# A two-block transformer kernel: a later silu on another load queue, a pace of the modulation steps by stage, and six smaller reorderings

## The chip, the core and the metric

The kernel runs on one core of a Trainium2 chip. A core has TensorE (PE: matmuls; PEld is its weight load), VectorE (DVE), ScalarE (ACT), GpSimd (POOL) and SyncE (SP), each with an instruction stream of its own, run in order; they meet through semaphores. Transfers between HBM and the core's memory are issued by SP or ACT here, each on a queue of its own, and are carried by 16 DMA engines. The metric is the device time of one execution in microseconds (us). In the trace every row has its engine, the line of the kernel it stems from, and the idle time ahead of it with what ended that.

## What is computed

Two blocks of two layers, float32 in and out, 256 tokens of width 1024. The parts that the change touches, cut:

```python
def mixer_block(h, ...):                       # block 1, both layers
    proj = (h @ w_in)                          # conv, retention, GLA and gate columns
    y_a = short_conv(cu, cb, cc, conv_w)
    y_b = head_norm(retention(rq, rk, rv), ret_gn_w, center=True) * silu(rg)
    gate_logits = ga_down @ gla_w_a2 + gla_b_a
    log_a = log_sigmoid(gate_logits) / 16
    y_c = head_norm(gated_linear_attention(gq, gk, gv, log_a), gla_gn_w) * silu(gr)
    merged = (sigmoid(gate_a) * (y_a @ w_branch_a) + sigmoid(gate_b) * (y_b @ w_branch_b)
              + sigmoid(gate_c) * (y_c @ w_branch_c))
    return merged @ w_out
# block 1, per layer: x += norm(mixer(norm(x)));  x += norm(swiglu(norm(x)))

# block 2, per layer, for a latent x and a context xc of 256 tokens each:
    mod_x = silu(c) @ ada_w[l] + ada_b[l]      # 6 x 1024 values; the same of c_ctx for the context
    hx = rmsnorm(x) * (1 + sc1) + sh1
    mix = conv branch, mLSTM, attention (8 query heads, 2 key heads of 64), gated, @ w_out
    x = x + g1 * mix
    x = x + g2 * conv_ffn(rmsnorm(x) * (1 + sc2) + sh2)
```

## The kernel before

Activations stay in on-chip memory, transposed: 1024 features as 8 tiles of 128, 256 tokens along the free axis, two tiles to a buffer (128x512). Only weights stream. A chunk of 128x1024 float32 (512 KB) is fetched on SP by `load` (L188; five buffers, `raw`); `halve` splits it into two float32r halves, `whi` on ACT (L197) and `wlo` on DVE (L199), and `mmT` runs 24 matmuls on it: high weight by high activation (L214), low by high (L218), high by low (L220). `mmK` (L228, L230, L232) is the same with the roles of the operands exchanged. So one chunk asks PE for 24 passes, ACT for one split, DVE for one.

Work is written down as a sequence of chunks; the scheduler of the framework orders each engine's instructions from it, with priorities (`high_priority`; `soon` is one of them) and explicit after-relations (`issue_after`). Side work (GLA decay and levels, retention, normalisations) runs in generators in lanes: `later` puts one in a lane, every chunk's `tick` moves each lane one step, `drain` runs a lane to its end.

Block 1, each layer: `b1_norm` splits the scaled input into `xh` and `xl` and forms the squares for the norm in `b1_norm_rest`; the mixer (L700 to 830) multiplies chunk after chunk of `w_in`, starts the lanes, then runs the branch stage (`gates`, `branch`: three branches of four column pairs, from L803 on), then `w_out`. `gla_decay` (L853) forms the decay from `ga` by the matmul `gl` (L866). `gla_scores` (L884) has eight levels; each makes E = exp(-|cum - ref| / 16) on DVE (L902, L903) and ACT (L904), the products `ql` (DVE, L906) and `kl` (POOL, L907), the matmuls `gs` (L922) and masked copies of them on DVE (L930). `gn_finish` (L935) normalises the heads: mean, square, variance, then `rsqrt` (L239 to L244), eleven DVE instructions on 128x4 values. The swiglu FFN follows, 22 column tiles and then `down`.

The modulation of block 2's layers is computed meanwhile, beside block 1: its input `silu` (128 x 2 x 1024, the vector repeated over partitions) is loaded on ACT's queue and made by tanh in `ada_prep` (L353). Each `ada_step` (L366) loads one 512 KB chunk of `ada_w` on SP, through the same five buffers, and runs two multiply-and-reduce instructions on DVE (L376), behind the latest `wlo`. `ada_beat` makes a step at every `ada_every`-th weight chunk; `ada_pace(n)` sets that number, up to a goal of 48 steps before block 2's first layer. Before: every second chunk in layer 0's FFN, every eighth in layer 1's mixer, every second in layer 1's FFN.

In block 2, an attention block of two heads (`r` = 0, 1) multiplies scores by values into one PSUM tile `po` (L1455), head r into partitions 64r to 64r+63, `nk` = 4 key tiles for the latent and 2 for the context; each matmul is two passes. The last FFN ends with four pairs of `down` (22 row tiles in three chunks by two column tiles), each followed by the residual (`b2_residual`, L1814) and a store.

## Time and profile before

| | us |
|---|---|
| median of 3 runs | 2595.44 |
| lowest, highest | 2587.75, 2596.06 |
| the profiled execution's own time | 2584.17 |
| its span in the profile | 2581.5 |
| PE busy | 2524.3 (98%) |
| DVE busy | 1949.0 (75%) |
| ACT busy | 1282.6 (50%) |
| POOL busy | 144.4 (6%) |

The span runs from the first to the last instruction of the trace; 2.7 us lie around it. Busy times are sums over the instructions of an engine. A row of the timeline gives the start, the length and, in brackets, the idle time of that engine just ahead of it. The windows give the same sums for a stretch, and the TensorE clock that was granted there (1.00 is 2.4 GHz, 0.50 is 1.2 GHz).

### The profile page before, as it was taken

To read this page: it belongs to the slowest core of one execution; us is meant where nothing else is said; L and a number is where in the kernel's file an instruction comes from. 1 tells how busy PE (TensorE), PEld (TensorE's weight loads), DVE (VectorE), ACT (ScalarE), POOL (GpSimd) and SP (SyncE) were. 2 spreads that over 40 slices of the span, in tenths; PEclk is the share of its full clock that TensorE was granted. 3 is DMA by queue.
4 is the path that set the end of the run, shared out by engine and by line. 5 is a ranking of instruction groups with operands and counts; after the bars stand their busy time and mean duration, and the time that the engine had idled before them with its cause. 6 is when DMAs were issued, how large, how long until landed. Compare 5 with 4: busy or idle time off the path is not lost. (4 is left out here: it accounts for less than half of the span.)

```text
span 2581.5 us, 44809 instructions
## 1 busy us (share of the span) xinstructions
PE 2524.3 (98%) x18010; PEld 2319.6 (90%) x18010; DVE 1949.0 (75%) x3254; ACT 1282.6 (50%) x2003; POOL 144.4 (6%) x151
## 2 busy tenths in 40 slices
PE   7999999999999999999999999999999999999999
PEld 7999999999999999888977679988889899999999
DVE  6987799699869958876884456975677674966994
ACT  5545544553454546343444534642345644665763
POOL 0100000010100001000010110000000000000000
PEclk9999999999999999999999999999999999999999
DMA  6545488554656754322333224434336333444554
GB/s 232 172 165 180 146 266 258 188 196 149 206 177 212 263 182 168 114 90 90 107 102 111 74 107 148 167 124 141 115 127 203 136 106 121 141 131 155 178 190 148
DMA packets 116209, 405.62 MB, mean 157 GB/s; under 512 B 12817, under 2 KB 16529, under 8 KB 116001
## 3 DMA queue, kind: packets, MB, share of 16 engines
q1 hardware_dynamic: 112880, 397.96, 46.0%
q10 hardware_dynamic: 3120, 4.80, 0.5%
q8 instruction: 141, 2.31, 0.4%
q14 instruction: 68, 0.55, 0.1%
HBM read 401.66 MB, written 1.05 MB: 156 GB/s over the span
## 5 line engine op out<-in xcount | busy, mean ns | idle before, releaser
L199 DVE TENSOR_TENSOR wlo<-raw,whi 128x1024 fp32r<-128x1024 f32 (+3 forms) x674 | 816.0, 1215 | 353.9 <-ACT whi L197 352.2
L197 ACT ACTIVATE whi<-raw 128x1024 fp32r<-128x1024 f32 (+3 forms) x674 | 697.7, 1040 | 591.8 <-PE pj L220 222.3
L214 PE MATMUL pj<-hh,whi 128*128 128x256 f32 (+1 forms) x3120 | 528.8, 311 | 5.5 <-ACT whi L197 4.0
L218 PE MATMUL pj<-hh,wlo 128*128 128x256 f32 (+1 forms) x3120 | 523.5, 309 | 4.3 <-DVE wlo L199 3.7
L214 PEld LDWEIGHTS pj<-hh,whi 128*128 128x128 f32 x3120 | 437.3, 188 | 46.2 <-ACT whi L197 5.2
L218 PEld LDWEIGHTS pj<-hh,wlo 128*128 128x128 f32 x3120 | 435.6, 189 | 43.4 <-DVE wlo L199 8.1
L220 PE MATMUL pj<-hl,whi 128*128 128x256 f32 (+1 forms) x2440 | 389.0, 296 | 0.0
L220 PEld LDWEIGHTS pj<-hl,whi 128*128 128x128 f32 x2440 | 329.6, 188 | 17.5 <-issue 0.3
L376 DVE CUSTOM_DVE_ANT_0 adr<-raw,silu 128x1024 bf16<-128x1024 f32 x192 | 238.1, 1245 | 0.5
L220 PE MATMUL pj<-kc,whi 128*128 128x512 f32 (+1 forms) x680 | 151.8, 344 | 0.0
L1263 DVE SCALAR_TENSOR_TENSOR dw<-z,hw,dw 128x512 f32<-128x512 f32 (+1 forms) x240 | 135.9, 609 | 0.2
L220 PEld LDWEIGHTS pj<-kc,whi 128*128 128x128 f32 x680 | 112.2, 188 | 16.7
L1821 ACT ACTIVATE fc<-pj,vecs 128x256 f32<-128x256 f32 (+1 forms) x78 | 52.0, 667 | 113.9 <-PE pj L220 111.3
L228 PE MATMUL pk<-whi,hh 128*128 128x256 f32 (+1 forms) x512 | 88.0, 291 | 0.0
L1822 DVE SCALAR_TENSOR_TENSOR fc<-pj,vecs,fc 128x255 f32<-128x255 f32 (+1 forms) x78 | 47.4, 609 | 48.7 <-ACT fc L1821 47.9
L230 PE MATMUL pk<-wlo,hh 128*128 128x256 f32 (+1 forms) x512 | 83.7, 283 | 0.0
L218 PE MATMUL dn<-fah,wlo 128*128 128x256 f32 (+1 forms) x440 | 76.5, 301 | 0.9 <-DVE wlo L199 0.9
L214 PE MATMUL dn<-fah,whi 128*128 128x256 f32 (+1 forms) x440 | 76.7, 301 | 0.0
L220 PE MATMUL dn<-fal,whi 128*128 128x256 f32 (+1 forms) x440 | 76.5, 300 | 0.1
L228 PEld LDWEIGHTS pk<-whi,hh 128*128 128x128 f32 x512 | 72.5, 190 | 3.0 <-issue 0.7
L255 POOL TENSOR_TENSOR sq<-sq,sq 128x512 f32<-128x512 f32 x15 | 25.2, 1681 | 855.5 <-ACT sq L252 642.8
L214 PE MATMUL pj<-yh,whi 128*128 128x256 f32 (+1 forms) x384 | 71.5, 313 | 0.0
(432 smaller groups left out, 3686.2 us busy)
## 6 DMA issues: line engine op xcount, KB each, us to landing
raw<-stream SPq DMA_DIRECT2D x620, 512.0 KB, 3.6
raw<-ada_stream SPq DMA_DIRECT2D x96, 512.0 KB, 3.9
raw<-stream SPq DMA_DIRECT2D x36, 384.0 KB, 3.5
raw<-stream SPq DMA_DIRECT2D x11, 408.0 KB, 3.2
raw<-stream SPq DMA_DIRECT2D x6, 272.0 KB, 2.7
xc<-xT SPq DMA_DIRECT2D x2, 512.0 KB, 5.6
xc<-cT ACTq DMA_DIRECT2D x1, 1024.0 KB, 10.9
silu<-c ACTq DMA_DIRECT2D x2, 512.0 KB, 12.6
```

The lines of the kernel that those rows point to most:

```text
L197: nc.scalar.activation(hi, raw, AF.Copy)
L199: self.mark = nc.vector.tensor_tensor(out=lo, in0=raw, in1=hi.bitcast(F32), op=ALU.subtract)
L214: mm(out, wh[:, k, cs], xh[k], start=first and k == 0, stop=False)
L218: mm(out, wl[:, k, cs], xh[k], start=False, stop=False)
L220: mm(out, wh[:, k, cs], xl[k], start=False, stop=last and k == kt - 1)
L228: mm(out, xh[k], wh[:, k, :], start=first and k == 0, stop=False)
L230: mm(out, xh[k], wl[:, k, :], start=False, stop=False)
L255: nc.gpsimd.tensor_tensor(out=sqs[0], in0=sqs[0], in1=sq, op=ALU.add)
L376: nc.vector.tensor_tensor_reduce(junk, raw, self.silu[:, s], 0.5, 0.0, ALU.mult, ALU.add, self.mods[:, l, n, s : s + 1])
L1263: V.scalar_tensor_tensor(d, src, w, d, ALU.mult, ALU.add)
L1821: A.activation(v(t), v(ps), AF.Identity, scale=w(1), bias=self.col(f"ffn_conv_b{l}", f + i))
L1822: V.scalar_tensor_tensor(v(t)[..., 1:256], v(ps)[..., 0:255], w(0), v(t)[..., 1:256], ALU.mult, ALU.add)
```

## The change

1. Six matmuls on constants are put at the head of PE's stream.
2. `ada_prep` is parted: the two `silu` loads (`ada_load`) stay where they were in the program but go to SP's queue; the tanh and the multiply move to the start of layer 0's branch stage.
3. The pace: every fourth chunk in the branch stages of both layers, every third in the FFNs, none in the rest of the mixers.
4. `b1_norm`: the `xl` instructions lose their priority, and the squares are put behind the last weight split on ACT (`self.high`).
5. GLA level: min(-e, e) on DVE becomes an Abs on ACT, with the sign in the scale of the Exp.
6. `gn_finish`: `rsqrt` on DVE becomes one power on POOL.
7. The value products of two heads alternate.
8. The last pair of `down` runs one column tile after the other; each is added and stored when it is done, the last in two halves on two queues.

```diff
@@ halve
-            nc.scalar.activation(hi, raw, AF.Copy)
+            self.high = nc.scalar.activation(hi, raw, AF.Copy)
@@ ada_prep
+    def ada_load(self):
+        for s in range(2):
+            self.nc.sync.dma_start(self.silu[:, s], self.d["c2"][s : s + 1].to_broadcast([128, 1024]))
...
-            v = self.silu[:, s]
-            nc.scalar.dma_start(v, self.d["c2"][s : s + 1].to_broadcast([128, 1024]))
...
@@ b1_norm, b1_norm_rest
-        with self.soon():
-            for j, (hi, lo) in enumerate(hl):
+        for j, (hi, lo) in enumerate(hl):
...
-        with self.soon():
+        with self.soon(), self.tc.issue_after(self.high.ins):
             parts = self.squares([self.x_pair(j) for j in range(4)])
@@ down
-    def down(self, l, j, H, L, name):
+    def down(self, l, j, H, L, name, done=None):
         ps = self.mm("dn")
+        if done:
+            for a in range(2):
+                p = ps[:, a * 256 : a * 256 + 256]
+                for r, kt in ((0, 8), (8, 8), (16, 6)):
+                    w = self.chunk(name, l, r * 128, kt, (2 * j + a) * 128, 128)
+                    self.mmT(p, w, H[r : r + kt], L[r : r + kt], first=r == 0, last=r == 16)
+                    self.tick()
+                done(a, p)
+            return
@@ mixer of block 1, start
-            self.ada_prep()
+            self.ada_load()
...
-        else:
-            self.ada_pace(8)
@@ mixer of block 1, ahead of the branch stage
+        if l == 0:
+            self.ada_prep()
+        self.ada_pace(4, 1)
@@ FFN of block 1
-        self.ada_pace(2, 1)
+        self.ada_pace(3, 1)
@@ gla_scores
-                V.scalar_tensor_tensor(e, e, -1.0, e, ALU.mult, ALU.min)
-                A.activation(e, e, AF.Exp, scale=1.0 / 16)
+                A.activation(e, e, AF.Abs)
+                A.activation(e, e, AF.Exp, scale=-1.0 / 16)
@@ gn_finish
-            self.rsqrt(y, v, 4)
+            nc.gpsimd.tensor_tensor(out=y, in0=v, in1=self.mhalf[:, 0:4], op=ALU.pow)
@@ attention
-            for r in range(2):
-                for k in range(nk):
+            for k in range(nk):
+                for r in range(2):
@@ last FFN of block 2
-        for j in range(4):
+        for j in range(3):
             ps = self.down(l, j, H, L, "ffn_w_down_2")
...
+        def done(a, ps):
+            k = 6 + a
+            for i in range(1 + a):
+                c = slice(256 * i // (1 + a), 256 * (i + 1) // (1 + a))
+                x = self.xc[:, k, c]
+                V.scalar_tensor_tensor(x, ps[:, c], self.mods[:, l, 40 + k, 0:1], x, ALU.mult, ALU.add)
+                (self.nc.scalar if i else self.nc.sync).dma_start(self.d["outT"][128 * k : 128 * k + 128, c], x)
+        self.down(l, 3, H, L, "ffn_w_down_2", done)
@@ start of the program
+            ps = self.aux("warm")
+            for _ in range(6):
+                nc.tensor.matmul(ps[:, 0:256], self.ones, self.one256, start=True, stop=True)
```

How the scheduler places this is seen at three places. First ACT in layer 0's mixer, some 25 to 50 us into the program: `whi` are splits, `gm`, `rmask` and `cT` loads of masks and of the context on ACT's queue, `ga` feeds the matmul `gl`. Before:

```order
L416 DMA xc<-cT 128x8x256 [waits DMAHW6_49]
L197 ACTIVATE whi_443<-raw_441 128x1024 [waits DMAHW4_49,PE_49]
L197 ACTIVATE whi_488<-raw_486 128x1024 [waits PE_49]
L709 ACTIVATE gv_416<-pk_152,rs_234 128x256 [waits Pool_49]
L709 ACTIVATE gv_416<-pk_153,rs_234 128x256 [waits DVE_49]
L357 DMA silu<-c 128x1024 [waits DMAHW0_49]
L357 DMA silu<-c 128x1024 [waits DMAHW2_49]
L197 ACTIVATE whi_525<-raw_523 128x1024 [waits PE_49]
L361 ACTIVATE adr_422<-silu 128x512 [waits DMAHW0_49]
L361 ACTIVATE adr_425<-silu 128x512 [waits DVE_49]
L361 ACTIVATE adr_429<-silu 128x512 [waits DMAHW2_49,DVE_49]
L361 ACTIVATE adr_432<-silu 128x512 [waits DVE_49]
L860 ACTIVATE ga_471<-ga_472 16x256 [waits DVE_49,PE_49]
```

After (the two loads of `silu` now stand in SP's stream, each between two weight loads):

```order
L415 DMA gm_350<-gmask 128x512 [waits DMAHW5_49]
L418 DMA kc_130<-rmask 128x512 [waits DMAHW6_49]
L418 DMA kc_131<-rmask 128x512 [waits DMAHW7_49]
L419 DMA xc<-cT 128x8x256 [waits DMAHW0_49]
L197 ACTIVATE whi_438<-raw_436 128x1024 [waits DMAHW3_49,PE_49]
L197 ACTIVATE whi_483<-raw_481 128x1024 [waits PE_49]
L721 ACTIVATE gv_423<-pk_159,rs_241 128x256 [waits Pool_49]
L721 ACTIVATE gv_423<-pk_160,rs_241 128x256
L197 ACTIVATE whi_520<-raw_518 128x1024 [waits PE_49]
L873 ACTIVATE ga_466<-ga_467 16x256 [waits PE_49]
```

The two loads and the four tanh no longer stand ahead of `ga`; the waits of the mask and context loads on DMA semaphores are on other semaphores than before, since the count of loads on each has shifted.

Second, DVE in the mixers, where `gn_finish` of a retention half (`var`, `rsh`, `on`) meets the masked copies `S` of a GLA level. Before:

```order
L199 TENSOR_TENSOR wlo_1744<-raw_1741,whi_1743 128x1024
L242 TENSOR_TENSOR rst_1570<-rsh_1569 128x4
L579 TENSOR_TENSOR yal_1585<-cy_1477,yah_1584 128x512
L243 SCALAR_TENSOR_TENSOR rst_1570<-rst_1570,var_1566 128x4
L947 TENSOR_TENSOR on_1619<-ro_1516,mu_1620 128x512
L244 SCALAR_TENSOR_TENSOR rsh_1569<-rst_1570,rsh_1569 128x4
L930 COPY_PREDICATED S_602<-Am_125,gs_1643 128x2x128
L242 TENSOR_TENSOR rst_1570<-rsh_1569 128x4
L930 COPY_PREDICATED S_603<-Am_125,gs_1643 128x2x128
L243 SCALAR_TENSOR_TENSOR rst_1570<-rst_1570,var_1566 128x4
L953 TENSOR_REDUCE var_1626<-sq_1624 128x4
L244 SCALAR_TENSOR_TENSOR rsh_1569<-rst_1570,rsh_1569 128x4
```

After:

```order
L199 TENSOR_TENSOR wlo_1717<-raw_1714,whi_1716 128x1024
L581 TENSOR_TENSOR yal_1569<-cy_1472,yah_1568 128x512
L960 TENSOR_TENSOR on_1603<-ro_1511,mu_1604 128x512
L943 COPY_PREDICATED S_597<-Am_132,gs_1616 128x2x128
L943 COPY_PREDICATED S_598<-Am_132,gs_1616 128x2x128
L966 TENSOR_REDUCE var_1610<-sq_1608 128x4
L943 COPY_PREDICATED S_597<-Am_132,gs_1617 128x2x128
L967 TENSOR_SCALAR var_1610<-var_1610 128x4
L943 COPY_PREDICATED S_598<-Am_132,gs_1617 128x2x128
L970 TENSOR_TENSOR on_1603<-on_1603,rsh_1613 128x512
```

The multiply chains of `rsqrt` between splits and copies are gone; `on` reads the `rsh` that POOL has written.

Third, PE at the first value products of the latent in block 2, with the scores of the next heads behind them. Before (x2 is two passes with the same head):

```order
L1455 MATMUL po_15752<-pT_15532,vt_13152 64x256 x2
L1455 MATMUL po_15752<-pT_15533,vt_13120 64x256 x2
L1455 MATMUL po_15752<-pT_15534,vt_13152 64x256 x2
L1455 MATMUL po_15752<-pT_15535,vt_13120 64x256 x2
L1435 MATMUL sc_15769<-kT_13153,qT_14324 128x256
```

After:

```order
L1468 MATMUL po_15671<-pT_15451,vt_13071 64x256
L1468 MATMUL po_15671<-pT_15453,vt_13071 64x256
L1468 MATMUL po_15671<-pT_15451,vt_13071 64x256
L1468 MATMUL po_15671<-pT_15453,vt_13071 64x256
L1468 MATMUL po_15671<-pT_15452,vt_13039 64x256
L1468 MATMUL po_15671<-pT_15454,vt_13039 64x256
L1468 MATMUL po_15671<-pT_15452,vt_13039 64x256
L1468 MATMUL po_15671<-pT_15454,vt_13039 64x256
L1448 MATMUL sc_15688<-kT_13072,qT_14243 128x256
```

The four key tiles are the same; `pT` of the two heads (`15451`, `15452` of the one, `15453`, `15454` of the other) now alternate from matmul to matmul.

## Rows read from the trace of the kernel before

**Rows 1.** Section 1 of the page: each engine's busy time, its share of the span, instructions.
```profile
PE 2524.3 (98%) x18010; PEld 2319.6 (90%) x18010; DVE 1949.0 (75%) x3254; ACT 1282.6 (50%) x2003; POOL 144.4 (6%) x151
```

**Rows 2.** Waits of TensorE over the span: total us, times, longest us.
```profile
PE pk L655 <- ACT xh L497: 8.8, 3, 7.5
...
PE gl L866 <- ACT ga L860: 3.7, 1, 3.7
...
PE gs L922 <- DVE rsh L244: 2.5, 1, 2.5
...
PE rsb L296 <- DVE dg L289: 2.4, 5, 0.5
...
PE st L273 <- DVE sq L259: 1.0, 3, 0.5
```

**Rows 3.** Timeline of ScalarE near the start: start, length, instruction, [idle before <- releaser].
```profile
42.54 1.15 ACT L361 ACTIVATE adr<-silu 128x512 f32<-128x512 f32 x2 [9.26 <-DMA silu<-c]
...
45.62 0.36 ACT L860 ACTIVATE ga<-ga 16x256 f32<-16x256 f32 x1
```

**Rows 4.** Timeline of TensorE over the same place.
```profile
46.02 2.07 PE L866 MATMUL gl<-ga,kc 16*128 16x256 f32 x4 [3.69 <-ACT ga L860]
...
48.02 1.22 PE L228 MATMUL pk<-whi,hh 128*128 128x256 f32 x4
```

**Rows 5.** Two stretches: length, busy time of each engine, granted clock, DMA share, GB/s.
```profile
45.50:52.34 6.84, 6.32 (x24) 5.48 (x25) 6.36 (x12) 5.09 (x8) 0.00 (x0) 0.50 0.36 118
...
612.10:618.96 6.86, 5.59 (x25) 5.39 (x26) 6.17 (x20) 0.74 (x2) 0.00 (x0) 0.50 0.23 76
```

**Rows 6.** DMA issues between 29 and 46 us: KB each, median us from issue to landing.
```profile
raw<-stream SPq DMA_DIRECT2D x4, 512.0 KB, 8.4
...
silu<-c ACTq DMA_DIRECT2D x2, 512.0 KB, 12.6
```

**Rows 7.** Timeline of TensorE at three waits in the two mixers of block 1.
```profile
113.00 0.70 PE L986 MATMUL rs<-r,r 128*128 128x256 f32 x2 [1.03 <-DVE r L746]
...
149.68 0.88 PE L965 MATMUL ot<-mats,on 128*128 128x128 f32 x6 [0.61 <-DVE on L957]
...
613.37 2.04 PE L922 MATMUL gs<-ql,kl 64*128 64x128 f32 x8 [2.47 <-DVE rsh L244]
```

**Rows 8.** Five stretches of block 1, columns as in group 5.
```profile
580.00:632.00 52.00, 48.27 (x386) 46.44 (x384) 48.94 (x98) 17.23 (x22) 4.47 (x5) 0.93 0.42 142
...
152.00:258.00 106.00, 106.00 (x947) 105.26 (x946) 78.20 (x113) 53.34 (x65) 9.47 (x7) 1.00 0.53 179
...
632.00:648.00 16.00, 15.91 (x143) 15.51 (x143) 16.00 (x27) 8.10 (x11) 1.48 (x3) 1.00 0.48 167
...
309.50:441.00 131.50, 125.23 (x1046) 121.05 (x1045) 121.83 (x168) 56.84 (x65) 0.00 (x0) 1.00 0.78 255
...
788.00:915.00 127.00, 123.94 (x1058) 122.41 (x1057) 114.56 (x164) 63.28 (x79) 2.00 (x2) 1.00 0.75 251
```

**Rows 9.** Groups of VectorE instructions in the FFN of layer 0: count, busy us, mean ns.
```profile
L376 DVE CUSTOM_DVE_ANT_0 adr<-raw,silu 128x1024 bf16<-128x1024 f32 x44 | 53.1, 1216 | 0.0
...
L199 DVE TENSOR_TENSOR wlo<-raw,whi 128x1024 fp32r<-128x1024 f32 (+1 forms) x44 | 52.9, 1208 | 8.6 <-ACT whi L197 8.4
```

**Rows 10.** Timeline of TensorE at one block of the latent's attention.
```profile
1421.00 2.86 PE L1455 MATMUL po<-pT,vt 128*64 128x256 f32 x16
...
1424.86 1.09 PE L1455 MATMUL po<-pT,vt 128*64 128x256 f32 x8
```

**Rows 11.** Three lines over the span: instructions, minimum, median and longest ns, first and last start.
```profile
L903 DVE SCALAR_TENSOR_TENSOR E<-E x16: 675/682/693, 62.9 to 652.5; 128x512 f32<-128x512 f32 x16
...
L281 POOL TENSOR_TENSOR rs<-ms,mhalf x29: 695/707/1632, 18.6 to 2399.3; 128x2 f32<-128x2 f32 x28, 128x4 f32<-128x4 f32 x1
...
L304 PE MATMUL warm<-one x56: 379/379/463, 285.2 to 967.0; 128*128 128x256 f32 x56
```

**Rows 12.** Timeline of VectorE at the end of the span.
```profile
2577.63 0.88 DVE L1814 SCALAR_TENSOR_TENSOR xc<-dn,mods,xc 128x256 f32<-128x256 f32 x2 [7.68 <-PE dn L220]
```

More of the change, by code (lines that the diff above doesn't have):

```diff
@@ L355, in ada_prep @@
         for s in range(2):
-            v = self.silu[:, s]
-            nc.scalar.dma_start(v, self.d["c2"][s : s + 1].to_broadcast([128, 1024]))
             for i in range(2):
                 th = self.u("adr")
-                x = v[:, 512 * i : 512 * i + 512]
+                x = self.silu[:, s, 512 * i : 512 * i + 512]
                 nc.scalar.activation(th, x, AF.Tanh, scale=0.5)
@@ L497, in b1_norm @@
                     A.activation(hi[:, sl], self.xc[:, k, 0:256], AF.Copy, scale=self.col(wname, k))
-        with self.soon():
-            for j, (hi, lo) in enumerate(hl):
-                for a in range(2):
-                    sl, k = slice(a * 256, a * 256 + 256), 2 * j + a
-                    V.scalar_tensor_tensor(lo[:, sl], self.xc[:, k, 0:256], self.col(wname, k), hi[:, sl].bitcast(F32), ALU.mult, ALU.subtract)
+        for j, (hi, lo) in enumerate(hl):
+            for a in range(2):
+                sl, k = slice(a * 256, a * 256 + 256), 2 * j + a
+                V.scalar_tensor_tensor(lo[:, sl], self.xc[:, k, 0:256], self.col(wname, k), hi[:, sl].bitcast(F32), ALU.mult, ALU.subtract)
         self.later("norm", self.b1_norm_rest(wname, st))
@@ L671, in turned @@
         return ps[0:16, 0:256]
-    def down(self, l, j, H, L, name):
+    def down(self, l, j, H, L, name, done=None):
         ps = self.mm("dn")
+        if done:
+            for a in range(2):
+                p = ps[:, a * 256 : a * 256 + 256]
[5 more added lines that the diff above has]
+            return
         for r, kt in ((0, 8), (8, 8), (16, 6)):
@@ L1993, in b2 @@
         if "b1" not in self.parts:
+            self.ada_load()
             self.ada_prep()
```

## The prediction

> **What bounds the kernel now.** The busy shares come first: PE is at 98% of the span, DVE at 75%, ACT at 50% [rows 1]. PE's own work is the same after the change but for the order of some passes, so what can be won is PE's idle time, 2581.5 − 2524.3 = 57.2 us, and the time in which PE runs at half clock or one head's passes run alone. The list of PE's waits says who ends the idle time [rows 2], and it is in small pieces: no wait but the start's 7.5 us is over 3.7. So I go stage by stage, and in each ask what DVE and ACT had to do, for these two end nearly all of it. The sums are made against the profiled execution (2584.17 us; 2.7 lie around its span); the median shown is 11.3 above it, and I carry that over. About 0.3%, some 8 us, is what a measurement of this kernel can tell from no change.
>
> **The silu load and tanh.** ACT stands at the first tanh for 9.26 us until the load of `silu` has landed; `ga` follows the four tanh at 45.62 [rows 3], and PE waits for `ga` 3.69 us at `gl` [rows 4]. After that wait the granted clock is 0.50, the 1.2 GHz level, from 45.5 to 52.34, with PE busy 6.32 us in it [rows 5]; half of that, 3.16, is the price of the clock. The loads take 12.6 us from issue to landing behind masks and the context on ACT's queue, while weight loads of the same size on SP's queue take 8.4 in those microseconds [rows 6]. After the change neither the loads nor the tanh stand ahead of `ga`, so 3.69 + 3.16 = **6.9** go. What is late next: the two `silu` loads take two places of 512 KB among SP's weight loads, and each delays the weight behind it by some 2 us; I give the first chunks enough lead for that. The tanh, four instructions, run later in the branch stage where ACT is half idle (53.34 of 106.00 us [rows 8]): nothing. The queue order has a catch. The issues of masks and of the context wait on DMA semaphores that, counted anew, belong to `silu` loads and weights; ACT runs in order, so the weight splits behind them wait too. That is the first rival.
>
> **Start, norms, warm matmuls.** Six matmuls are twelve passes of 0.38 us at most at the full clock (L304) [rows 11], twice that at half, so at least 4.6 and at most 9 us against 7.5 us in which PE waits for the first activations [rows 2]: free, or up to 1.5 lost. If they bring the clock up earlier, a part of the first ten microseconds is won, but these wait for loads. I take **0.5**, between −1.5 and 2.5. In the norms PE waits for squares and diagonals, 1.0 and 2.4 us in all [rows 2]; the new order of `xl` and squares may save or lengthen either: **1.0**, between −1 and 3.4.
>
> **rsqrt on POOL, Abs on ACT.** Eleven small DVE instructions per `gn_finish` half become one POOL power of 0.7 us (L281) [rows 11], and the 16 L903 of 0.68 us [rows 11] leave DVE for ACT. In layer 0's mixer the waits for a DVE chain that stood behind such work are 1.03 and 0.61 [rows 7]: **1.6**. In layer 1's mixer DVE also carried steps of the modulation, and from 580 to 632 it is busy 48.94 of 52.00 while PE idles 52.00 − 48.27 = 3.73 [rows 8]; 2.47 of this is one wait for the end of an `rsqrt` chain [rows 7], and after it PE was busy 5.59 us at half clock [rows 5], which costs 2.8. The early mixer has no step of the modulation any more: 3.7 + 2.8 = **6.5**. Against it stand 16 Abs of at least the Exp's kind on an ACT that is busy 17.23 of 52 there [rows 8]; they lie beside other work, but in order with the weight splits (last rival).
>
> **The pace.** In layer 0's FFN PE is busy 125.23 of 131.50, so 6.27 us idle, and DVE 121.83 [rows 8]. 44 multiply-and-reduce instructions of 1.22 us there are 22 steps, beside 44 splits of 1.21 [rows 9]. A step in every third chunk makes about 15 steps: 14 × 1.22 = 17 us less on DVE, which falls to 80% of the stretch, and a third less of the extra load. PE's idle time there is small waits for splits; I take **5.5** of 6.27. In layer 1's FFN it is 127.00 − 123.94 = 3.06 [rows 8], and I take **2.6**. The steps that leave go to the branch stages: nine in layer 0's, 9 × 2 × 1.22 = 22 us of DVE in a stretch where it is busy 78.20 of 106.00 and PE never idles [rows 8]: DVE goes to 95% at most. That this can be borne is shown by 632 to 648, where DVE is busy all 16.00 us and PE still 15.91 [rows 8]. But it is the end of the margin: **−1.0** for this and **−1.5** for small new waits elsewhere, between 0 and −8 (as much as the FFNs lose now).
>
> **Value products in turns.** The latent's block of 16 passes takes 2.86 us, the context's of 8 takes 1.09 [rows 10]. One pass of 256 columns (L304) lasts 0.379 [rows 11]. If the 8 run as four pairs, a pair follows the other after (1.09 − 0.379) / 3 = 0.24 us; at 0.22 to 0.24, 16 passes as eight pairs would take 1.9 to 2.04, and 16 one by one 3.6 to 3.9. So before, the passes of the second head already run partly beside the first's (2.86), though the order has all of one head first. In turns I take 1.95, 0.9 less, in 8 blocks (four in each layer of block 2): **7.2**. The context's blocks are paired already: nothing.
>
> The Trainium skill has a rule on this: by the page "TensorE: Matmul & The Clock Gate", Part 3 (Packing small matmuls), passes on different column tiles overlap, but matmuls start and end strictly in program order. By that rule the heads, one after the other, could meet only at the border, a block before would take about 3.6, and turns would win 1.7 in each of 8, 13.4 in all, which would make the time 2559.4. The trace speaks against it: 2.86, and 1.09 for 8 passes that also stand head after head [rows 10]. I go by the trace.
>
> **The end.** The last additions take 0.88 us after PE's end [rows 12], then the store. By tile, the first half is done under the last matmuls, and the last store is a quarter as large: **0.5**, between 0 and 1.5.
>
> **Sum.** 6.9 + 0.5 + 1.0 + 1.6 + 6.5 + 5.5 + 2.6 + 7.2 + 0.5 − 2.5 = 29.8 us. Against the profiled execution: 2584.2 − 29.8 = 2554.4. Against the median: 2595.4 − 29.8 = **2565.6**.
>
> **Rivals**, all against the median:
> - *The silu load stays late.* For it: an issue on ACT now waits on the semaphore of the second `silu` load, with weight splits queued behind; if that load takes 12.6 us again, ACT stands still about as long as before, and of 7.4 (silu and start) 1.5 remain. Against it: weights on SP's queue take 8.4 [rows 6], and less when ACT's big loads are not yet under way. 2565.6 + 5.9 = 2571.5.
> - *Turns give nothing.* For it: PE overlaps two heads by itself, and alternating weight loads may cost what pairing brings. Against: the 8-pass blocks. 2565.6 + 7.2 = 2572.8.
> - *The FFNs keep their waits.* For it: with 255 GB/s and a DMA share of 0.78 [rows 8] the loads themselves may be late, or ACT's splits. Against: DVE is at 93%, and two chunks cost it 2 × 1.21 + 2 × 1.22 + some 0.9 of other work, as long as PE's 48 passes. Without the 8.1: 2573.7.
> - *Slower: Abs holds ACT.* Abs waits for DVE's subtraction (L902) at each of 16 GLA levels, and the next weight splits are queued behind it on ACT; before, ACT waited there only for L903's end. If a wait like that of 613.37 comes of it, with its clock, it costs 2.47 + 2.8 = 5.3 us. From 29.8 / 5.3, the sixth of 16, the kernel is slower than before; with eight, 2565.6 + 42 = 2608. For it: E's latency grows by an ACT instruction; against it: L903 ended before ACT as well, and a level has four chunks of time.
> - *The strict order* of above: 2559.4.
>
> **How the numbers follow.** Forecast 0.55; silu late 0.08; turns nothing 0.10; FFN waits stay 0.11; strict order 0.06; two or three of the first rivals together, with costs at their bounds, 0.07 (all three: 2565.6 + 5.9 + 7.2 + 8.1 = 2586.8, within 0.3% of before); Abs 0.03. Faster by over 0.3%: 0.55 + 0.08 + 0.10 + 0.11 + 0.06 = 0.90; within 0.3%: 0.07; slower: 0.03. The range: below, costs at nothing (2.5), strict order (6.2), start, norms and end at their upper bounds (2.0 + 2.4 + 1.0) and some of the 7.7 by which the runs of before reach below their median: 2548. Above, two rivals together and costs of −8 (5.5 more): 2565.6 + 13.1 + 5.5 = 2584.
>
> **What would show it.** In the profile after: `gl` starts near 42 with no wait over 1 us and no half clock behind it; ACT's wait before a `whi` at 30 us stays under 3; no PE wait for `rsh` in layer 1's mixer and no half clock at 612; PE idle in the FFNs under 1.5 us together with DVE near 80%; PE idle in the branch stages under 1; `po` x16 near 1.95. The prediction is wrong if the branch stages idle by 5 us or more, if ACT is the releaser of PE's waits at the GLA levels, or if `po` stays at 2.8.

## The result and the profile after

The changed kernel takes 2550.97 us in the median (2548.15 to 2557.70), the kernel before 2594.94 (2587.75 to 2596.06). These medians are 44 us apart. The ratio of the runs' means is 0.984, with an interval from 0.9814 to 0.9867: about 41 us less, 34 to 48. Six kernels that differ from the changed one by a small edit, each measured beside further runs of the kernel before (medians from 2587.84 to 2589.63), have ratios from 0.984 to 0.985, so 40 us is what to go by. The time lies in the range (2548 to 2584), at its lower end; against the forecast of 2565.6 it is 14.6 us lower. The profiled executions stand closer together than the medians: spans of 2581.5 and 2547.4, 34.1 us apart, since the profile of before (2584.17) was 11 us under its median and that of after (2549.96) lies at its own.

Section 1 of the page of after, as [rows 1]:

```profile
PE 2510.3 (99%) x18022; PEld 2313.0 (91%) x18022; DVE 1929.6 (76%) x3151; ACT 1289.9 (51%) x2017; POOL 154.1 (6%) x159
```

PE is busy 14.0 us less, with twelve more passes, and idle 2547.4 − 2510.3 = 37.1 us instead of 57.2. Less idle time alone is 20.1 us. Of the other 14.0, the value products that run in pairs are some 7; the rest is a balance of passes that are no longer at half clock or held up behind a wait, and of passes that came at a slower interval (both below). Where both went is read from the start of the same PE instruction in both traces; each row is the change within one stage, by their differences:

| stage of the program | start of its end mark, before and after | change | forecast |
|---|---|---|---|
| start to first retention scores | 113.00, 106.60 | −6.4 | −6.9 −0.5 −1.0 |
| rest of layer 0's mixer, first branches | 218.61, 211.43 | −0.8 | −0.6 |
| other branches, `w_out` | 286.67, 278.99 | −0.5 | +1.0 for the branch stages of both layers |
| norm and FFN of layer 0 | 474.14, 458.44 | −8.0 | −5.5, norms −0.5 |
| mixer of layer 1 up to its second branch | 647.34, 623.94 | −7.7 | −6.5 |
| other branches, `w_out` | 765.30, 741.32 | −0.6 | in the +1.0 above (new waits anywhere: +1.5) |
| norm and FFN of layer 1 | 964.92, 934.36 | −6.6 | −2.6, norms −0.5 |
| block 2 up to the first value products | 1421.00, 1392.05 | +1.6 | 0 |
| up to the last value products | 2344.47, 2308.56 | −7.0 | −7.2 |
| to PE's end | 2577.59, 2544.13 | +2.5 | 0 |
| behind PE's end | 2581.5, 2547.4 | −0.6 | −0.5 |

The lines of after that answer to [rows 8] (FFN of layer 0, of layer 1, branch stages of layer 0 and 1; length, busy time of each engine, clock, DMA share, GB/s), and to [rows 10] (value products):

```profile
292.00:423.00 131.00, 131.00 (x1111) 130.91 (x1112) 118.00 (x155) 64.45 (x75) 0.00 (x0) 1.00 0.75 246
754.90:881.90 127.00, 126.62 (x1111) 126.33 (x1110) 116.28 (x163) 69.47 (x88) 2.27 (x1) 1.00 0.74 243
134.80:250.40 115.60, 115.60 (x1031) 114.86 (x1029) 105.32 (x139) 61.11 (x78) 15.59 (x10) 1.00 0.66 219
624.30:739.00 114.70, 113.24 (x996) 111.91 (x994) 89.58 (x111) 58.58 (x75) 13.82 (x9) 1.00 0.66 223
```

```profile
1392.05 1.95 PE L1468 MATMUL po<-pT,vt 128*64 128x256 f32 x16
...
1394.99 1.08 PE L1468 MATMUL po<-pT,vt 128*64 128x256 f32 x8
```

PE has next to no waits left in the FFNs (0.38 us in layer 1's window), the branch stages bear their new steps (in layer 0 DVE is busy 105.32 of 115.60 us and PE is idle for none of it), and the 16 passes take the 1.95 that the prediction named. But the first two windows also show a thing that the prediction did not have: the same 1111 passes take 131.00 us in one FFN and 127.00 in the other, and in the slower one PE never idles.

### The profile page after: what moved, and what is told of

It reads as the page before. It is cut to its first block, busy times and chain, and to the rows that moved or that the text cites. A ratio compares the mean times of both kernels' runs of the same rounds, so it can differ in the third digit from the quotient of the medians.

```text
span 2547.4 us, 44751 instructions
## 1 busy us (share of the span) xinstructions
PE 2510.3 (99%) x18022; PEld 2313.0 (91%) x18022; DVE 1929.6 (76%) x3151; ACT 1289.9 (51%) x2017; POOL 154.1 (6%) x159
## 4 chain that ended last, share of the span: by engine, by line
PE 85%; DVE 8%; ACT 3%; issue 2%; DMA 1%; POOL 1%; ACTq 0%; DVEq 0%; POOLq 0%; SPq 0%
PE pj L214 19%; PE pj L220 19%; PE pj L218 19%; PE dn L220 4%; PE dn L218 4%; PE dn L214 4%; DVE wlo L199 2%; PE pk L228 2%; PE pk L232 2%; PE pk L230 2%; PE pv L1647 2%; PE ms L1607 1%; DVE dw L1276 1%; PE br L214 1%; PE br L220 1%
## 5 line engine op out<-in xcount | busy, mean ns | idle before, releaser
L230 PEld LDWEIGHTS pk<-wlo,hh 128*128 128x128 f32 x512 | 70.4, 189 | 3.4 <-DVE wlo L199 3.4
```

Source lines behind the costliest of these rows:

```text
L230: mm(out, xh[k], wl[:, k, :], start=False, stop=False)
```

## The experiments

Times are ratios to the kernel before, measured beside it, with their intervals; what a run tells is read from the stages of its profile, against the kernel named. A profile's own span is one execution, and the intervals of the passes (below) alone can move it by 5 to 10 us, so medians and profiles differ.

### The silu load: one part alone, and the part undone

`e_silu`, the kernel before with part 2 alone:

```diff
-            nc.scalar.dma_start(v, self.d["c2"][s : s + 1].to_broadcast([128, 1024]))
+            self.nc.sync.dma_start(self.silu[:, s], self.d["c2"][s : s + 1].to_broadcast([128, 1024]))
...
-            self.ada_prep()
+            self.ada_load()
...
+        if l == 0:
+            self.ada_prep()
         for j in range(4):
             branch(0, j, yA, gates(0, j))
```

> The kernel before with part 2 alone (silu loaded on SyncE's queue, tanh at the branch stage), which is the step that the prediction put at 6.9 us. Theory of the prediction: no wait of TensorE for ga, no half clock from 45 to 52, rs about 6.9 us earlier (106). Theory M (the mask's cast ahead of a weight split on VectorE takes its place): a wait of 1 to 3 us for wlo near 33 to 38 with half clock behind it, rs 2 to 4 us earlier. Rival (the loads between the weights make weights late): rs less than 1 us earlier.

0.9961 (0.9946 to 0.9975), some 10 us. PE's timeline:

```profile
41.31 1.12 PE L871 MATMUL gl<-ga,kc 16*128 16x256 f32 x4
```

No wait ahead of `gl`, which starts at 41.31 instead of 46.02 [rows 4], and no half clock; the first retention scores start at 104.15 instead of 113.00, without the 1.03 us wait [rows 7]. By itself the part is worth 8.9 us there: the 6.9 of the prediction, and the wait at 113 that the prediction had put on L903. From `gl` to the scores PE waits for nothing and takes 62.84 us.

`e_oldsilu`, the changed kernel with part 2 undone:

```diff
-            self.nc.sync.dma_start(self.silu[:, s], self.d["c2"][s : s + 1].to_broadcast([128, 1024]))
+            self.nc.scalar.dma_start(self.silu[:, s], self.d["c2"][s : s + 1].to_broadcast([128, 1024]))
...
             self.ada_load()
+            self.ada_prep()
...
-        if l == 0:
-            self.ada_prep()
         self.ada_pace(4, 1)
```

> The changed kernel with part 2 undone: silu loaded on ScalarE's queue and made early, in the place of the kernel before. The changed kernel's trace has a wait of 3.16 us at 34.02 for a weight split that stands on VectorE behind the cast of a mask that has not landed, so the silu wait may only have changed places. Theory S (silu's load and tanh were the price): gl comes 3 to 6 us later again and the first masked level with it, + 4 to 6 us against the changed kernel. Theory M (the masks are the limit, the silu part alone gives little, and the gain of the first 50 us came from the warm matmuls' clock): within 2 us of the changed kernel at that place.

0.9845 (0.9816 to 0.9873), and the first retention scores at 106.94 against 106.60. ACT waits for the silu load nearly as long as before, and PE has no wait ahead of `gl`; first ACT's timeline, then PE's:

```profile
39.21 1.15 ACT L364 ACTIVATE adr<-silu 128x512 f32<-128x512 f32 x2 [7.45 <-DMA silu<-c]
```

```profile
33.33 1.20 PE L230 MATMUL pk<-wlo,hh 128*128 128x256 f32 x4 [2.57 <-DVE wlo L199]
...
43.28 1.13 PE L878 MATMUL gl<-ga,kc 16*128 16x256 f32 x4
```

So in these executions a part that is worth 8.9 us there by itself is worth 0.3 beside the others. The changed kernel has the wait for `wlo` at that place too. Its PE timeline and, behind it, DVE's:

```profile
34.02 0.74 PE L230 MATMUL pk<-wlo,hh 128*128 128x256 f32 x4 [3.16 <-DVE wlo L199]
```

```profile
30.10 0.43 DVE L416 CAST Am<-gm 128x512 uint8<-128x512 f32 x1 [1.18 <-DMA gm<-gmask]
32.41 0.43 DVE L416 CAST Am<-gm 128x512 uint8<-128x512 f32 x1 [1.88 <-DMA gm<-gmask]
32.75 2.36 DVE L199 TENSOR_TENSOR wlo<-raw,whi 128x1024 fp32r<-128x1024 f32 x2
```

PE comes to this chunk nearly three microseconds earlier than before (30.15 instead of 32.90), and meets a split that stands on DVE behind the cast of a mask whose load has not landed.

### What bounds the start

`e_mask`, the changed kernel with the casts written later, the loads left:

```diff
-            nc.vector.tensor_copy(self.gmask[:, 4 * i : 4 * i + 4].rearrange("p a t -> p (a t)"), t)
+            self.gm.append(t)
...
+        if l == 0:
+            for i, t in enumerate(self.gm):
+                V.tensor_copy(self.gmask[:, 4 * i : 4 * i + 4].rearrange("p a t -> p (a t)"), t)
         rv = []
```

> The changed kernel with one move: the two casts of the GLA mask on VectorE (L416) are written after the second value chunk instead of right behind their loads; the loads stay. Theory M (the 3.16 us wait of TensorE at 34.02 and the half clock behind it come from the weight split queued on VectorE behind a cast that waits for the mask's load to land at 32.39): that wait falls under 0.5 us, no half clock near 35, and gl with all that follows comes 3.5 to 5 us earlier. Rival (the weight's own load is late: the load issued at 26.54 landed only at 33.08): the wait moves one or two chunks on and keeps over 2 us.

0.9845 (0.982 to 0.9869). `gl` starts 4.4 us earlier, no wait stands at 34 and no half clock behind it, as theory M expected. But the edit can't be credited with it. The casts still ran ahead of the two splits in question, and the second could start at 29.81 instead of 32.41, because in this execution the mask's load had landed earlier. DVE's timeline of `e_mask` and, behind it, of `e_tail` (below), whose instructions stand in the changed kernel's order on every engine:

```profile
29.81 0.43 DVE L738 CAST Am<-gm 128x512 uint8<-128x512 f32 x1 [0.23 <-DMA gm<-gmask]
```

```profile
29.02 0.84 DVE L416 CAST Am<-gm 128x512 uint8<-128x512 f32 x2
```

In `e_tail` the wait at 34 is gone without any edit there, and `gl` starts at 39.26. In `e_kick` (below), again with the same order up to 307 us, the second cast starts at 33.57, PE waits 3.89 us and `gl` starts at 45.60. So the wait goes with the landing of the mask's load, which differs by some four microseconds between executions; what the order of the casts is worth is not shown.

All that `e_mask` gains is given back by 108: the first retention scores start at 108.37, 1.8 later than in the changed kernel, behind new waits for splits, of which the first is

```profile
58.91 1.19 PE L218 MATMUL pj<-hh,wlo 128*128 128x256 f32 x8 [2.08 <-DVE wlo L199]
```

and another is 2.26 at 75.98. `e_tail` has such waits too, 1.87 at 58.59 and 1.28 at 72.02, and the three executions of one order, with `gl` at 39.26, 43.76 and 45.60, reach the scores at 106.76, 106.60 and 107.01.

`e_nowarm`, the changed kernel without the six matmuls of part 1:

```diff
-            ps = self.aux("warm")
-            for _ in range(6):
-                nc.tensor.matmul(ps[:, 0:256], self.ones, self.one256, start=True, stop=True)
```

> The changed kernel without part 1 (the six matmuls at the start). Theory (the start's gain is the clock: with them half clock ends at 10.8 instead of 18.2): half clock again until 16 to 18 us, the first norm's statistics (st, 16.70) 0.5 to 1 us later and the ga transposes (30.01) 1 to 2.5 us later; the wait at 34 shrinks by as much, since the mask lands when it does, so that behind it at most 1 us remains of the difference. Rival (they cost nothing and bring nothing): the ga transposes within 0.5 us.

0.9849 (0.9831 to 0.9866). Half clock lasts until 14.0 (PE's passes are 0.23 us apart until there and 0.12 behind it), the statistics start at 15.73 instead of 16.70 and the scores at 105.63, 1.0 earlier: the matmuls bring nothing here. `e_norm` is the kernel before with part 4 alone, `e_oldnorm` the changed kernel with part 4 undone:

```diff
-        with self.soon():
-            for j, (hi, lo) in enumerate(hl):
+        for j, (hi, lo) in enumerate(hl):
...
-        with self.soon():
+        with self.soon(), self.tc.issue_after(self.high.ins):
             parts = self.squares([self.x_pair(j) for j in range(4)])
```

> The kernel before with part 4 alone (splits ahead of squares). The first product with the first retention scores behind it (rs) starts at 113.0 in the kernel before and at 106.6 in the changed one, and neither the silu part undone (106.9) nor the warm matmuls left out (105.6) gives that back. Theory N (part 4 is what moves the start: the second weight split is no longer behind four squares on ScalarE): the wait of 2.56 us at 13.12 falls to about 0.6, rs comes 3 to 5 us earlier. Rival O (no part alone does it: the waits on loads, masks and silu stand behind each other): rs within 1.5 us of the kernel before, the wait for ga at gl grows by what the start gains.

> The changed kernel with part 4 undone. Theory N: rs 3 to 5 us later than in the changed kernel, the wait of 2.5 us for the second split near 13 is back. Rival O: rs within 1.5 us. In the other norms (both layers, ahead of FFN and mixer) both expect under 0.5 us, net of TensorE's pass interval.

`e_norm`: 0.9993 (0.998 to 1.0006), scores at 113.62. The wait for the second split falls from 2.56 to 0.48, and the wait for `ga` takes it over, with half clock from 42.6 to 52.8:

```profile
45.56 2.07 PE L865 MATMUL gl<-ga,kc 16*128 16x256 f32 x4 [5.59 <-ACT ga L859]
```

`e_oldnorm`: 0.984 (0.9815 to 0.9865), scores at 106.25. The scores move by 0.6 us or less in either kernel: rival O. A difference of a microsecond or two can't be told here: without any wait the stretch from `gl` to the scores takes 62.84 us in the changed kernel and 61.42 in `e_kick`, by the interval of the passes alone.

The changed kernel and seven versions of it, with different waits ahead, reach the retention scores between 105.6 and 108.7. Where `gl` comes at 39 to 40 (`e_mask`, `e_tail`, and `e_best` below), the way from there to the scores takes 67.5 to 69.0 us, with 3.5 to 6.5 us of waits, most of them for a split on DVE. Where it comes at 42.8 to 45.6 (the changed kernel, `e_nowarm`, `e_kick`), PE waits for nothing on that way (1.0 to 1.3 us in `e_oldnorm` and `e_oldsilu`, with `gl` at 43.5 and 43.3), and DVE has little room: in the changed kernel's trace it is busy 43.8 of the 45 us from 60 to 105. So what is won ahead of `gl` comes back as waits for splits behind it. `e_silu` with 104.15 is the one below; it is ahead of the changed kernel by 2.45 us at `gl` already, since it doesn't have the wait at 34, and it has neither Abs nor power. Whether the new placement of the GLA levels makes the waits of an early `gl` is not shown by a run made for it.

### Pace, and ACT and POOL for DVE

`e_pace`, the kernel before with part 3 alone:

```diff
-        else:
-            self.ada_pace(8)
...
+        self.ada_pace(4, 1)
         for j in range(4):
             branch(0, j, yA, gates(0, j))
...
-        self.ada_pace(2, 1)
+        self.ada_pace(3, 1)
```

> The kernel before with part 3 alone (pace by stage). Theory: layer 0's FFN with its norm 7.5 to 8 us shorter, layer 1's 5 to 6.6, as between the two traces; the layer 1 mixer 7 us shorter by theory P (no steps there), under 2 by theory L (rsqrt chain). The branch stages lose under 1 us. In all 20 (P) or 14 (L). Rival (loads are what the FFNs wait for): FFN idle time of TensorE stays over 4 us in layer 0.

`e_lanes`, the kernel before with parts 5 and 6 alone:

```diff
-                V.scalar_tensor_tensor(e, e, -1.0, e, ALU.mult, ALU.min)
-                A.activation(e, e, AF.Exp, scale=1.0 / 16)
+                A.activation(e, e, AF.Abs)
+                A.activation(e, e, AF.Exp, scale=-1.0 / 16)
...
-            self.rsqrt(y, v, 4)
+            nc.gpsimd.tensor_tensor(out=y, in0=v, in1=self.mhalf[:, 0:4], op=ALU.pow)
```

> The kernel before with parts 5 and 6 alone (Abs on ScalarE, power on GpSimd); the modulation steps stay where they were, one in eight chunks of the layer 1 mixer. Theory L (the waits of the mixers come from the rsqrt chain and L903 on VectorE): the layer 1 mixer, from the ga transposes to its second conv branch product, gets 6 to 7.6 us shorter, with no wait for rsh and no half clock at 612, and layer 0's 2.0; 8 to 10 us in all. Theory P (they come from the modulation steps that ran there): at most 3 us in the layer 1 mixer, the layer 0 mixer 1 to 2. Either way the FFNs stay within 1 us. Rival of the prediction (Abs holds ScalarE): new waits for weight splits at the GLA levels of over 2 us each.

`e_pace`: 0.9914 (0.9888 to 0.994), some 22 us, the largest of the parts; `e_lanes`: 0.996 (0.9946 to 0.9974), some 10. The stretch of layer 1's mixer that [rows 8] show from 580 to 632, and FFN 0, in `e_pace`, and the same mixer stretch in `e_lanes`:

```profile
307.50:432.00 124.50, 124.50 (x1060) 124.50 (x1059) 110.67 (x144) 58.73 (x68) 0.00 (x0) 1.00 0.78 254
```

```profile
571.00:623.00 52.00, 51.34 (x440) 49.91 (x440) 50.22 (x105) 20.97 (x26) 4.53 (x7) 1.00 0.44 139
```

```profile
580.50:632.50 52.00, 50.64 (x426) 49.38 (x425) 48.71 (x84) 20.76 (x27) 5.94 (x8) 0.97 0.46 143
```

Before, PE passed 386 instructions there and idled 3.73 us. Either part alone takes most of it: the mixer from the `ga` transposes to the second branch gets 4.3 us shorter with the pace alone and 4.7 with the lanes alone, and 7.6 with both. So the two gains are not a sum: 9.0 apart, 7.6 together. Nor are they alike. With the pace alone one wait of 0.66 us is left and no half clock, but the passes come at the slower interval (below), 786 of 886 instead of 237 of 865; that is some 2.4 us, without which the pace alone would bring 6.7, near the 7 of theory P. With the lanes alone a wait and half clock stay, where theory L expected none:

```profile
611.30 1.13 PE L922 MATMUL gs<-ql,kl 64*128 64x128 f32 x8 [1.36 <-DVE on L947]
...
612.96 1.92 PE L218 MATMUL pj<-hh,wlo 128*128 128x256 f32 x8
```

The FFNs belong to the pace: 8.0 us with the norm in layer 0, 2.8 in layer 1, where the slower interval hides some 2.6 more; in `e_lanes` neither gets shorter. At layer 0's GLA levels PE has no new wait for a split in `e_lanes`, so the Abs does not hold it up there.

### The value products

`e_po`, the kernel before with part 7 alone:

```diff
-            for r in range(2):
-                for k in range(nk):
+            for k in range(nk):
+                for r in range(2):
```

> The kernel before with part 7 alone (value products of two heads in turns). Theory: the change is local; each of the 8 blocks of 16 passes falls from 2.79 us (start to start of the next row) to 1.88, as in the changed kernel, and nothing else moves: 8 x 0.91 = 7.3 us less, a ratio of 0.997. Rival (strict program order, a serial block would be 3.6): the block before is already at 2.79, so the rival would only hold if the block after came below 1.88; and a second rival, that PE's next wait takes the gain back, would leave the scores behind each block waiting, with less than 4 us won in all.

0.9985 (0.9971 to 0.9998). From the start of a block to the next row, seven of the eight blocks fall from 2.79 to 1.88, the eighth is cut in two by other passes (0.58 and 1.87): 6.7 us. Its profiled span is nonetheless 2584.1, longer than before: stages that the change doesn't touch are longer, the last FFN alone by 3.5 ahead of `down` and 2.4 in it, where PE idles no more than before. This led to the next run.

### The interval of the passes

In both FFNs of block 1 the same instructions run on the same shapes. PE's timeline of after, first layer 0, then layer 1:

```profile
321.88 1.10 PE L214 MATMUL pj<-hh,whi 128*128 128x256 f32 x8
322.83 1.10 PE L218 MATMUL pj<-hh,wlo 128*128 128x256 f32 x8
...
783.42 1.07 PE L214 MATMUL pj<-hh,whi 128*128 128x256 f32 x8
784.33 1.07 PE L218 MATMUL pj<-hh,wlo 128*128 128x256 f32 x8
```

From start to start eight passes take 0.942 us in one and 0.907 in the other: 117.8 and 113.3 ns a pass, at full clock in both. Over the whole trace the intervals gather at these two values. `e_kick`, the changed kernel with ten single matmuls in layer 0's FFN:

```diff
+            if l == 0 and j:
+                nc.tensor.matmul(self.aux("kick")[:, 0:2], self.ones, self.m1024, start=True, stop=True)
```

> The changed kernel with ten single matmuls of 2 columns put between the chunks of layer 0's FFN, one for each column pair; it is more work, its output is not used. In the changed kernel's trace the passes of this FFN follow each other every 117.8 ns from 292 to 462 us, without a break, while layer 1's FFN with the same instructions runs at 113.3. Theory K (TensorE's pass interval has two levels; it falls into one at a disturbance and keeps it until the next): some of the stretches between two of these matmuls run at 113.3 and some at 117.8, the FFN gets up to 4 us shorter less some 0.1 to 0.2 us for each matmul. Rival (the interval is set by what else is busy in that stage, loads or VectorE): all of them stay at 117.8 and the FFN gets 1 to 2 us longer.

0.9847 (0.9829 to 0.9865), and the result is not clean: the interval fell to 113.3 at 302.5, behind two passes that were held up (174 and 221 ns) and ahead of the first of the ten matmuls, and stayed through all ten of them. `e_nowarm` and `e_tail`, where nothing is changed in this FFN, had 113.3 there as well (3.8 and 4.1 us less for the FFN up to `down`), `e_mask` and `e_oldsilu` 117.8 like the changed kernel. That the level belongs to the stage's load is ruled out: one and the same stage shows both. The clearest single change is in `e_best`, whose timeline has one such matmul between two chunks:

```profile
308.04 1.10 PE L218 MATMUL pj<-hh,wlo 128*128 128x256 f32 x8
308.98 1.10 PE L220 MATMUL pj<-hl,whi 128*128 128x256 f32 x8
309.93 0.28 PE L850 MATMUL kick<-m,one 128*128 128x2 f32 x2
310.06 1.16 PE L214 MATMUL pj<-hh,whi 128*128 128x256 f32 x8
311.07 1.07 PE L218 MATMUL pj<-hh,wlo 128*128 128x256 f32 x8
311.97 1.07 PE L220 MATMUL pj<-hl,whi 128*128 128x256 f32 x8
```

From start to start, eight passes take 0.94 ahead of it and 0.90 to 0.91 from 311.07 on. So there is one clean change from slow to fast at such a matmul, and at eleven others (ten in `e_kick`, the second in `e_best`) the interval was fast and stayed so; behind the third in `e_best` a wait follows at once. It is a state that a break in the stream can change. That the matmul always makes it fast is not shown. And it changes without a break too. In block 1's FFNs the first 48 passes of each pair of `down` come at 117 to 120 ns in the median in every trace, whatever the interval around them; in `e_best` the next ones are fast again, with PE idle for nothing and no other matmul between:

```profile
412.81 1.11 PE L220 MATMUL dn<-fl,whi 128*128 128x256 f32 x8
413.76 1.07 PE L214 MATMUL dn<-fh,whi 128*128 128x256 f32 x8
```

So the place in the program has a part in it as well; what sets the interval stays open.

### The last pair, and a version of it all

`e_tail`, the changed kernel with a PSUM tile for each half of the last pair:

```diff
-                p = ps[:, a * 256 : a * 256 + 256]
+                p = (ps if a == 0 else self.mm("dn"))[:, 0:256]
```

> The changed kernel with the last pair's second column tile in a PSUM tile of its own. In the changed kernel TensorE waits 0.67 us at 2536.12 for VectorE's addition of the first half, and the passes after it run at the slower interval. Theory: that wait goes, and from the start of the third down pair to TensorE's end it is 0.9 to 1.2 us less, so that the tail of part 8 becomes a gain of 0.6 instead of a loss. Rival: the wait comes from the split of the next chunk, and stays.

0.9844 (0.9815 to 0.9872). In the changed kernel the second half's first passes stand behind the addition of the first half:

```profile
2536.12 1.18 PE L214 MATMUL dn<-fah,whi 128*128 128x256 f32 x8 [0.67 <-DVE xc L1913]
```

In `e_tail` this wait is gone, and the passes behind stay at the faster interval: the last four pairs take 60.0 us as in the kernel before, not 61.2.

`e_best` is the changed kernel without part 1, with the silu loads issued some 40 us later, the edit of `e_tail`, and one matmul of two columns in each of three FFNs:

```diff
+            with self.tc.issue_after(self.fetch.ins):
+                self.ada_load()
...
+            if j == 1:
+                nc.tensor.matmul(self.aux("kick")[:, 0:2], self.ones, self.m1024, start=True, stop=True)
```

> The changed kernel with four edits: no warm matmuls (part 1 left out); the silu loads issued behind the loads of the retention keys, some 40 us later; the last pair's second tile in a PSUM tile of its own; and one matmul of 2 columns behind the second column pair of each of the three latent-only FFNs, to bring TensorE to its faster pass interval, as ten of ten did in the run before. Expected against the changed kernel: start 1 to 4 us less (loads of 1 MB leave the first 40 us, in which the DMA engines are busy 95%), last pair 2.0 less, FFN stretches at 113.3 ns a pass behind the small matmul: up to 4 us where the changed kernel's profile had 117.8. A span of 2535 to 2541 in the profile. If the interval is drawn anew at each disturbance and not set fast by the small matmul, one of the three FFNs stays at 117.8.

(That expectation counts ten matmuls as having made the interval fast; as said above, it was fast already.) 0.9815 (0.9801 to 0.983), 2542.43 us, from 2540.74 to 2544.62; the changed kernel beside its own runs of before has 0.984, and the intervals overlap. The span is 2539.6. All three FFNs run at 113.3 (in the changed kernel two of them did), the last pair is 1.2 shorter, but the start is 2.1 longer, not shorter: the scores begin at 108.71, with the DMA engines relieved (their share from 38 to 46 us is 0.54 instead of 0.90). So the load wasn't it. PE has four waits between 59 and 77; ACT's timeline at the first two:

```profile
58.02 0.63 ACT L920 ACTIVATE E<-E 128x512 f32<-128x512 f32 x1 [3.49 <-DVE E L919]
58.56 0.58 ACT L738 ACTIVATE rv<-pk 128x512 f32<-128x512 f32 x1
59.15 1.28 ACT L921 ACT_TABLE_LOAD   x1
60.45 0.63 ACT L921 ACTIVATE E<-E 128x512 f32<-128x512 f32 x1
60.98 1.99 ACT L197 ACTIVATE whi<-raw 128x1024 fp32r<-128x1024 f32 x2
```

ACT stands at an Abs for DVE's subtraction, and two weight splits come only behind it, a table load and the Exp. This is the mechanism of the prediction's slower rival, at one level instead of six. That it makes PE's waits here was not taken apart by a run. None of `e_best`'s own edits is needed for them: `e_tail` has waits at two of these places, with ACT standing at the same Abs for 3.08 us, while in the changed kernel ACT stands there for 2.34 and PE doesn't wait. What `e_best` and `e_tail` share is an early `gl` (40.22 and 39.26).

## Why the prediction was right, and where its sizes were off

The direction, the range and the list of stages held; the sum was 29.8, the profiles are 34.1 apart and the medians 44. That the sum came within 4.3 of the profiles is in part luck: the FFNs, the mixer of layer 1 and costs that didn't come were 10 better than forecast, while the start, block 2 and the way to PE's end were 6 worse. What makes the medians stand further apart than the profiles no trace shows. Point by point:

- **Silu, 6.9.** As a single edit it is right and measured (`e_silu`). As a term of the sum it was wrong: in the changed kernel it is worth 0.3 (`e_oldsilu`). The step that failed is "what is late next": the prediction looked for it in the weights behind the silu loads, and named a queue at which ACT would wait; it was a split on DVE, in the changed kernel behind the mask's cast (3.16 us), in `e_tail`, where the mask was in time, behind other work of DVE near 58 and 72. The start got 6.4 shorter, which looks like the forecast, but no single part holds it.
- **Start, norms, 0.5 and 1.0.** No gain that a run shows: without the warm matmuls the scores start 1.0 earlier, with part 4 alone 0.6 later, and without it, in the changed kernel, 0.35 earlier.
- **Mixer of layer 1, 6.5.** Measured 7.7 in the profiles. Pace and lanes each bring more than half by itself, and the pace, at an equal interval of the passes, nearly all.
- **FFNs, 5.5 and 2.6.** That the waits go with the steps was right, the term was too small: 8.0 and 6.6 in the profiles. A wait costs more than the idle time that the row shows. In the kernel before the row behind such a wait and the next one read

```profile
333.89 1.20 PE L214 MATMUL pj<-hh,whi 128*128 128x256 f32 x8 [0.63 <-ACT whi L197]
335.15 1.20 PE L218 MATMUL pj<-hh,wlo 128*128 128x256 f32 x8
336.19 1.07 PE L220 MATMUL pj<-hl,whi 128*128 128x256 f32 x8
```

  From 333.89 to 335.15 eight passes take 1.26 us, the next eight 1.04, where 0.907 is the interval without a wait: a further 0.35 and 0.13 us beside the 0.63 that counts as idle, since PE is booked as busy while a pass is held up. So 6.27 us of idle time was the lower part of the cost, and the prediction took less than all of it. Against this, layer 0's FFN fell to the slower interval: its passes cost some 4.5 us more than before in this profile, and none of that in other runs; in layer 1 the interval gave some 1.8. At an equal interval the two won some 12 and 5 us.

  The reason that the prediction gave did not come, though. DVE was to fall to 80% of the stretch; it is at 118.0 of 131.0 us, 90%, and PE passes more chunks in the time. A step takes DVE's time, one of the five buffers and a load of 512 KB. In the kernel before ACT waits 56.1 us for weight loads in that window, in `e_pace` 31.2 in a window of the same length. `e_pace` takes all three away together, so which of them made PE's waits stays open.
- **Branch stages, +1.0 and +1.5.** They cost nothing; they got 0.5 and 0.6 shorter.
- **Value products, 7.2.** 6.7. The trace's reading (the second head runs partly beside the first) was right, and the strict order of the Trainium skill's page "TensorE: Matmul & The Clock Gate", Part 3, which would have brought 13.4, is not what the 2.79 and 1.88 show.
- **The end, 0.5.** Behind PE's end 0.6 is won, as forecast; ahead of it 1.2 is lost by a wait that the prediction did not see: both halves lie in one PSUM tile, and the second half's passes wait until the first half is read. The rest of the 2.5 in the table is for the most part passes at the slower interval.
- **Block 2, 0.** 1.6 us went into half clock behind a wait that was there before. PE's timeline, before and then after:

```profile
996.41 0.31 PE L1528 MATMUL gt<-mats,m 36*128 36x36 f32 x2 [1.21 <-DVE m L1515]
...
997.34 1.07 PE L218 MATMUL pj<-hh,wlo 128*128 128x256 f32 x8
```

```profile
965.86 0.31 PE L1541 MATMUL gt<-mats,m 36*128 36x36 f32 x2 [1.22 <-DVE m L1528]
...
966.83 1.92 PE L218 MATMUL pj<-hh,wlo 128*128 128x256 f32 x8
```

  The same wait, 1.21 and 1.22; behind the one the clock stays, behind the other eight passes take 1.92. `e_oldsilu` and `e_tail`, with the same wait, keep the full clock there.

The rivals: silu late did not come as described, though a wait of 3.16 us did, by another load and on DVE. Turns and FFN waits were clearly refuted. Abs holding ACT came at a level or two at most, far from six.

## What to carry to other kernels

Ask of every wait that is removed what stands next at that place on the other engines, and take one part alone as well as one part undone: here one edit was worth 8.9 us alone and 0.3 beside the others. Where PE is fed in order, the idle time in a list of waits was the lower bound here of what the waits cost, since the passes behind them are booked as busy and stretched. A single profile's span can be off by some microseconds that no edit made; compare stage by stage, and count passes against time. And before an edit is credited with a wait that is gone, look at the same place in other traces with the same order of instructions there: the wait at 34 came and went without an edit.

## What the runs showed of the hardware

- TensorE's passes of 256 columns come at two intervals, 113.3 and 117.8 ns, at full clock and with the same instructions. The gate and up passes of an FFN kept one of them in a trace for 100 us and more, and changed it where another matmul stood between them or passes were held up; the passes of `down` change it without that. In one FFN of some 1100 passes it makes up to 4 us; summed over the changed kernel's trace the slower passes (115 to 121 ns) cost some 23 us against all at 113.3, in `e_best` some 16.
- The load of the mask, issued in the same order of instructions, landed in time for a cast at 29.4 us in one execution and at 33.6 in another.
- The same wait of PE is followed by 3.4 us at half clock in one execution and by none in another. Of the waits at the same four places (0.5 to 2.1 us long, at 277, 966, 1278 and 2371 us in the changed kernel) half clock followed two in the changed kernel, two in `e_oldsilu` and none in `e_best`; each time it costs 1.6 to 1.7 us.
